# Two-layer diffusion backbone: modulation rows one by one and at 1024 elements, opening and final norm reordered

## The chip, the cores and the metric

The kernel runs on one core of a Trainium2 chip. The metric is the device time of one launch in microseconds (us); lower is better. Each kernel was run three times, and the median is what is compared. Times inside the kernel come from one execution that was recorded by the hardware profiler.

## The reference

Two layers work on 640 tokens of width 1024: 128 context tokens and 512 latents. The even layer mixes tokens with a pooling and a gated convolution, the odd one with grouped-query attention; each is followed by a SwiGLU FFN of inner width 2816. Before each of the four sub-layers stands a norm with a modulation, and its output is gated:

```python
def ada_params(cvec, w_ada, b_ada):
    m = jax.nn.silu(cvec) @ w_ada + b_ada
    return jnp.split(m[:, None, :], 6, axis=-1)
def modulate(x, g, shift, scale):
    return rms_norm(x, g) * (1 + scale) + shift
def swiglu(h, w_in, w_out):
    a, b = jnp.split(h @ w_in, 2, axis=-1)
    return (jax.nn.silu(a) * b) @ w_out
...
    for l in range(DEPTH):
        sh1, sc1, g1, sh2, sc2, g2 = ada_params(c, w_ada[l], b_ada[l])
        h = modulate(x, norm_g[l, 0], sh1, sc1)
        ...
        x = x + g1 * y
        h = modulate(x, norm_g[l, 1], sh2, sc2)
        x = x + g2 * swiglu(h, w_ffn_in[l], w_ffn_out[l])
    y_sample = rms_norm(x, final_g)
```

In the left-out line `y` is the mixer's or the attention's output. Context tokens take their modulation from `c_ctx`, latents from `c`, so each of the 2 x 6 modulation vectors is needed for two conditions. All is float32.

## The kernel before

**Layout.** `x` stays on the core, transposed: 128 partitions, 8 blocks of 128 features, 640 tokens (`T`) in two halves of 320 (`HT`). Each weight block is loaded raw by the one DMA queue that SP issues, in program order, and split in a high and a low part: ScalarE (ACT) makes the high one (L144), VectorE (DVE) the low one (L145). A product of two split operands is three matmuls on TensorE (PE): high-high, high-low, low-high (`THREE`).

**FFN.** The 22 blocks of inner features run in three groups of 8, 8 and 6 (`GROUPS`). A group has an input part (`fi0_0` is layer 0's first) and an output part (`fo0_0`), whose eight steps end with a residual on VectorE (L506). In group 0 four blocks are multiplied plainly (eight steps, L289), the other four, and all of groups 1 and 2, by a scheme with seven products per unit of one block (`fast_blocks`, L630); the last operation of a unit on VectorE before its result is split is L652. A call `each(i)` stands behind step i, `fast_each(gi, n, p)` behind product p of unit n in group gi.

**Modulation rows.** Of the 96 block rows of modulation (2 layers x 6 vectors x 8 blocks) twelve are made on PE, in chunks of four: chunks 2 and 3 (the first sub-layer's scale) and 0 (half of its shift), by `ada_pe` (L306, with the condition as the small operand), `ada_row` (L324, a copy by ACT) and `ada_turn` (L330, tiny matmuls that turn the row into a column, tile `adat`). The other 84 rows are made on VectorE: a row is 128 partitions x 1024 weights (512 KB, tile `rawa`), multiplied with silu of each of the two conditions (`silb`) and summed along the way, in pieces of 512 elements (L371, tile `junk` takes the products): four pieces a row. Rows are jobs of four or eight; behind a job's last row the two halves are added (L385) and a bias is added (L392). `ada` holds 76 rows, `gates` the last 8 (layer 1's FFN gate). `ada.run(n)` puts n rows at that place of the program; the load of a later row follows each row. `EARLY` is the number of rows made before the first FFN; six row buffers there, two later.

**Order.** The opening is written out by hand and emitted in that order on every engine (`manual_schedule`); elsewhere a scheduler places the instructions of each engine by the program's order and its own readiness, but rows are held in program order among the rest (`keep_in_program_order`). On the chip each engine takes its instructions in order.

**Opening.** `prep(k)` makes block k of the first operand, x times scale, in both parts (ACT L483, VectorE L485); blocks 0 to 3 need chunk 2 (`sc`), blocks 4 to 7 chunk 3. `first_mm(m, ks)` multiplies blocks `ks` into output block m of the first projection (`pi`). `nrm.add` squares and sums x for the norm, with `pool_only` both on POOL. L474 is the first VectorE step of that norm behind its row pieces; the norm is applied by the `ev` multiply behind each projection step (L521; L526 copies its last columns on ACT). The pooling mixer follows (L904 and around).

**Tail.** Behind the last projection the final norm is made in two spans of 384 and 256 tokens, then `out` multiplies x with it block by block (L1446), and stores two blocks at a time.

Of the kernel before, what the change touches and what calls it, by code (L numbers as in the profile page):

```python
# [15 lines left out]
P = 128  # L16
D = 1024
# [19 lines left out]
EARLY = 30  # L37
# [23 lines left out]
def hybrid_step(  # L61
# [277 lines left out]
    class AdaDve:  # L339
# [17 lines left out]
        def run(self, rows, hold=True):  # L357
            for _ in range(rows):
# [7 lines left out]
                if b == 0:  # L366
                    self.got = self.rest.tile([P, 8, 2, 2], F32, tag="got", bufs=2, name=f"got_{l}_{b0}")
                for c in range(2):
                    for q in range(2):
                        cols = slice(512 * q, 512 * q + 512)  # L370
# [12 lines left out]
                if b == n - 1:  # L383
                    two = self.got[:, 0:n]
                    V.tensor_tensor(out=two[:, :, :, 0], in0=two[:, :, :, 0], in1=two[:, :, :, 1], op=ALU.add)  # L385
                    ada_done(l, b0, two[:, :, :, 0])
# [114 lines left out]
    def update(m, l, gate0, parts):  # L501

        assert (l, gate0 // 8, 8) in known
# [169 lines left out]
    def ffn(l, xin, hid, each=None, last=None, spare=None, fast_each=None):  # L673
# [37 lines left out]
        for gi, (f0, f1) in enumerate(GROUPS):  # L711
# [21 lines left out]
            if plain:  # L733
                project(f"fi{l}_{gi}", xin, KB, 2 * plain, in_done, ext=True, each=each and (lambda i: each(i, True)))
# [4 lines left out]
            if gi < len(GROUPS) - 1:  # L739
                project(f"fo{l}_{gi}", hid, f1 - f0, KB, lambda k, ps: residual(ps, k, l, 40), each=each)  # L740
# [5 lines left out]
    with tc.tile_pool(name="pool1", bufs=1) as p1:  # L746
# [3 lines left out]
        junk = p0.tile([P, 512], F32, tag="junk", name="junk")  # L750
        ada_raw = []

        def ada_load(ch):
# [8 lines left out]
            [(0, 4, 4)] + [(0, 8 * p, 8) for p in (2, 4, 3, 5)] + [(1, 8 * p, 8) for p in (1, 0, 2, 4, 3)]  # L762
# [5 lines left out]
        nc.sync.dma_start(x[:, 0:4, :], xT[:, 0:4, :])  # L768
        ada_load(3)
        ws.load(1, cut=True)  # L770
# [26 lines left out]

        acc = {ch: ada_acc(ch) for ch in (2, 3)}
        ada_pe(2, acc[2], range(4))
        row = ada_row(2, acc[2])  # L800
        ada_pe(3, acc[3], range(1))
        ada_turn(2, row)
        ada_pe(3, acc[3], range(1, 4))
        for k in range(4):
            nrm.add(k, pool_only=True)
        prep(0, bufA, 0, 0)
        prep(1, bufA, 0, 0)
        prep(2, bufA, 0, 0)
        ws.split(0, ahead=False)
        row = ada_row(3, acc[3])  # L810
        prep(3, bufA, 0, 0)
        ws.split(1, ahead=False)
        first_mm(0, range(0, 2))
        ada_turn(3, row)
        first_mm(0, range(2, 4))
        first_mm(1, range(4))
# [3 lines left out]
        for k in range(4, 8):  # L820
            nrm.add(k)
        first_mm(0, range(4, 8))
        first_mm(1, range(4, 8))
        ada.run(2, hold=False)
# [189 lines left out]
        for m in range(3):  # L1014
# [9 lines left out]
            each=lambda i: ada.run(1 + (i < 7) - (i >= 11)),  # L1024
# [19 lines left out]
        with tc.tile_pool(name="pool4", bufs=1) as p4:  # L1044
# [9 lines left out]
                each=lambda i, plain=False: ada.run(int(i >= 5) if plain else 1 + i % 2),  # L1054
# [550 lines left out]
```

## Time and profile before

| | before |
|---|---|
| runs, us | 1377.27, 1378.74, 1377.84 |
| median, us | 1377.84 |
| profiled execution, us | 1376.99 |
| its span, us | 1375.2 |
| mean granted PE clock | 0.986 |
| busy: PE / PEld / DVE / ACT / POOL | 97% / 94% / 79% / 46% / 5% |
| largest PE groups (share of the ending chain) | fi L630 24%, fo L289 21%, fi L289 7% |
| row pieces L371 | 336 pieces, 237.0 us of VectorE |

PE does matmuls, PEld the loads of their stationary operand. All times below are us from the start of the span, in the form: start, length, engine, line, operation, output <- inputs, shape, count, and in brackets how long the engine was idle before and what ended that.

### The profile page before, as it was taken

The numbers are of one execution on the slowest core, as the hardware profiler recorded it, in microseconds if no ns is written. First come the engines' busy times: TensorE is split into PE (matmuls) and PEld (weight loads), VectorE is DVE, ScalarE is ACT, GpSimd is POOL, SyncE is SP. The second block draws the span as 40 slices with busy tenths as digits, with TensorE's granted clock in tenths as the row PEclk, the third lists the DMA queues.
The fourth block names the chain that finished last, engine by engine and source line by source line (L and its number), as shares of the span: only waits on it lengthen the run. The fifth ranks groups of instructions, "written<-read, shape, count | busy, mean of one in ns | idle before, by whom it ended". The sixth has DMA issues, their size and how long they took to land.

```text
span 1375.2 us, 22538 instructions
## 1 busy us (share of the span) xinstructions
PE 1327.7 (97%) x8929; PEld 1294.1 (94%) x8929; DVE 1081.2 (79%) x2182; ACT 636.3 (46%) x1155; POOL 70.3 (5%) x73
## 2 busy tenths in 40 slices
PE   6989999989999999999999999999999999999995
PEld 3889999989999999999998899999999999999995
DVE  4899988999988898789976777689993577446745
ACT  3532335744135531454565675477551255314543
POOL 3200000000000000000013121000000000000013
PEclk7999999999999999999999999999999999999998
DMA  9635523134533254324531110031242122311212
GB/s 363 250 117 176 195 93 123 64 106 169 172 123 114 95 187 154 108 92 140 188 95 55 43 49 34 32 134 53 106 154 77 62 76 78 123 62 62 77 47 77
DMA packets 36872, 155.54 MB, mean 113 GB/s; under 512 B 4000, under 2 KB 11168, under 8 KB 26016
## 3 DMA queue, kind: packets, MB, share of 16 engines
q1 hardware_dynamic: 36768, 154.12, 32.2%
q8 instruction: 70, 1.15, 0.3%
q14 instruction: 34, 0.28, 0.1%
HBM read 148.60 MB, written 2.88 MB: 110 GB/s over the span
## 4 chain that ended last, share of the span: by engine, by line
PE 77%; DVE 16%; ACT 3%; issue 2%; DMA 1%; SPq 0%; POOL 0%; DVEq 0%; ACTq 0%; POOLq 0%
PE fi L630 24%; PE fo L289 21%; PE fi L289 7%; PE pq L289 5%; PE pi L289 5%; DVE junk L371 5%; PE po L289 4%; DVE wl_fi_p L145 3%; PE wb L289 2%; PE wa L289 2%; PE o L1326 2%; PE s L1276 1%; PE t L1309 1%; ACT wh_fi_p L144 1%; DMA raw_ada<-wada 1%
## 5 line engine op out<-in xcount | busy, mean ns | idle before, releaser
L144 ACT ACTIVATE wh_fi_p<-raw_fi 128x512 fp32r<-128x512 f32 x252 | 153.9, 626 | 219.5 <-PE fi L630 108.6
L371 DVE CUSTOM_DVE_ANT_0 junk<-rawa,silb 128x512 f32<-128x512 f32 x336 | 237.0, 705 | 6.5 <-DMA rawa<-wada 2.2
L145 DVE TENSOR_TENSOR wl_fi_p<-raw_fi,wh_fi_p 128x512 fp32r<-128x512 f32 x252 | 170.1, 686 | 64.1 <-ACT wh_fi_p L144 63.9
L506 DVE SCALAR_TENSOR_TENSOR x<-fo,mod,x 128x128 f32<-128x128 f32 (+1 forms) x144 | 55.5, 433 | 94.1 <-PE fo L289 90.8
L144 ACT ACTIVATE wh_fo<-raw_fo 128x1024 fp32r<-128x1024 f32 (+1 forms) x48 | 47.5, 990 | 145.4 <-PE fo L289 121.2
L630 PE MATMUL fi<-bh,wh_fi_p 128*128 128x320 f32 x288 | 89.0, 309 | 0.7 <-DVE x L506 0.5
L630 PE MATMUL fi<-bh,wl_fi_p 128*128 128x320 f32 x288 | 88.9, 309 | 0.6 <-DVE wl_fi_p L145 0.6
L630 PE MATMUL fi<-ah,wl_fi_p 128*128 128x320 f32 x288 | 88.8, 308 | 0.0
L630 PE MATMUL fi<-al,wh_fi_p 128*128 128x320 f32 x288 | 88.7, 308 | 0.0
L630 PE MATMUL fi<-ah,wh_fi_p 128*128 128x320 f32 x288 | 88.4, 307 | 0.0
L630 PE MATMUL fi<-bl,wh_fi_p 128*128 128x320 f32 x288 | 88.4, 307 | 0.0
L289 PE MATMUL fo<-al,wh_fo 128*128 128x320 f32 x352 | 80.8, 310 | 0.0
L289 PE MATMUL fo<-ah,wh_fo 128*128 128x320 f32 x352 | 80.6, 310 | 0.1
L289 PE MATMUL fo<-ah,wl_fo 128*128 128x320 f32 x352 | 80.4, 309 | 0.0
L289 PE MATMUL fo<-bh,wh_fo 128*128 128x320 f32 x328 | 75.2, 310 | 0.0
L289 PE MATMUL fo<-bh,wl_fo 128*128 128x320 f32 x328 | 75.0, 310 | 0.0
L289 PE MATMUL fo<-bl,wh_fo 128*128 128x320 f32 x328 | 74.9, 310 | 0.0
L630 PE MATMUL fi<-x0h,wh_fi_p 128*128 128x320 f32 x216 | 69.0, 323 | 5.0 <-DVE uv L652 3.6
L630 PE MATMUL fi<-xh,wh_fi_p 128*128 128x320 f32 x216 | 68.0, 320 | 2.6 <-DVE uv L652 2.1
L630 PE MATMUL fi<-x0l,wh_fi_p 128*128 128x320 f32 x216 | 66.9, 311 | 0.0
L630 PE MATMUL fi<-x0h,wl_fi_p 128*128 128x320 f32 x216 | 66.9, 311 | 0.0
L289 PE MATMUL pi<-ah,wh_in 128*128 128x320 f32 (+1 forms) x256 | 62.3, 326 | 4.7 <-ACT ev L526 3.8
(375 smaller groups left out, 3808.7 us busy)
## 6 DMA issues: line engine op xcount, KB each, us to landing
raw_fi<-wfi SPq DMA_DIRECT2D x44, 1024.0 KB, 4.8
rawa<-wada SPq DMA_DIRECT2D x84, 512.0 KB, 3.4
raw_fo<-wfo SPq DMA_DIRECT2D x16, 1024.0 KB, 4.9
raw_ada<-wada SPq DMA_DIRECT2D x12, 512.0 KB, 9.9
raw_in<-win SPq DMA_DIRECT2D x6, 1024.0 KB, 6.4
raw_fo<-wfo SPq DMA_DIRECT2D x8, 768.0 KB, 4.2
raw_qkv<-wqkv SPq DMA_DIRECT2D x6, 1024.0 KB, 5.0
raw_out<-wout SPq DMA_DIRECT2D x4, 1024.0 KB, 4.8
```

The costliest lines, as they stand in the source:

```text
L144: S.activation(h, src, AF.Copy)
L145: eng.tensor_tensor(out=l, in0=src, in1=h.bitcast(F32), op=ALU.subtract)
L289: PE.matmul(ps[:, h, 0 : hi - lo], w[a][:, k, cols], rhs[b][:, k0 + k, lo:hi], start=k == 0 and a == b, stop=k == kn - 1 and a == 1,)
L371: op = V.tensor_tensor_reduce(out=self.junk, in0=raw[:, cols], in1=self.silb[:, c, cols], scale=1.0, scalar=0.0, op0=ALU.mult, op1=ALU.add ...
L506: V.scalar_tensor_tensor(out=xs, in0=got[:, 0 : b - a], scalar=mod[l][:, gate0 + m, c : c + 1], in1=xs, op0=ALU.mult, op1=ALU.add,)
L630: PE.matmul(out, w[a][:, k, :], ops.get(OPERAND[p], b)[:, k, :], start=fresh and k == 0 and a == b, stop=k == ops.kn - 1 and a == 1, skip_ ...
L1276: PE.matmul(self.ps[:, hf, 0:HT], bufB[a][:, self.h, q0 : q0 + P], kt[b][:, self.kv, hf * HT : hf * HT + HT], start=n == 0, stop=n == 2,)
L1309: PE.transpose(flat(pt)[:, s * P : s * P + P], self.pe[:, s * P : s * P + P], ident)
L1326: PE.matmul(po[:, 0 : 2 * P], vt[a][:, self.kv, s * P : s * P + P], got[b][:, s, :], start=s == 0 and n == 0, stop=s == 4 and n == 2,)
```

## The change

- A row is split by the width of the tile that takes the products. The early one is now 1024 wide, so the 28 rows ahead of the first FFN (`EARLY`, 30 before) are two pieces each instead of four and need no addition of halves; later rows keep pieces of 512.
- The rows of the two FFN gate vectors (part 5 of each layer) are jobs of one row: addition and bias follow each row, and a residual asks only for its own block's row.
- Opening: the first projection's weights are loaded ahead of chunk 3's rows; dummy matmuls of zeros (128x512, into a bank that is free then) are put on PE in three places (6, 3 and 14); `ada_turn` of chunk 2 no longer stands behind chunk 3's first matmul; all four first `prep`s come ahead of chunk 3; the squares go from POOL to ACT and their sums from POOL to VectorE.
- FFN of layer 0: no rows in group 0's input part (seven before); fewer and more in the output parts (group 0 as before, `1 + i % 2`; group 1 two a step from the third step on); one in each unit of groups 1 and 2 (in every second before).
- Layer 1: the eight rows of `gates` move from the fast units of group 0 to the steps of `fo1_0`, one each, the first two loads ahead of the FFN.
- Tail: `out` multiplies four blocks in one operation on VectorE (it was one block at a time, a third on POOL) and stores them at once: two stores per span instead of four. The first half of the first span is put ahead of the second span's work. `nrm.finish` there is at raised priority.

```diff
@@ -34,7 +34,7 @@
 PLAIN = 4
 RAW = 3
 
-EARLY = 30
+EARLY = 28
 WINDOWS = (2, 4, 8, 16)
 PAD = 8
 UL = PAD + CTX + PAD + LAT + PAD
@@ -365,9 +365,10 @@
                 self.at += 1
                 if b == 0:
                     self.got = self.rest.tile([P, 8, 2, 2], F32, tag="got", bufs=2, name=f"got_{l}_{b0}")
+                n_part = D // self.junk.shape[-1]
                 for c in range(2):
-                    for q in range(2):
-                        cols = slice(512 * q, 512 * q + 512)
+                    for q in range(n_part):
+                        cols = slice(D // n_part * q, D // n_part * (q + 1))
                         op = V.tensor_tensor_reduce(
...
@@ -382,7 +383,8 @@
                             tc.keep_in_program_order(op)
                 if b == n - 1:
                     two = self.got[:, 0:n]
-                    V.tensor_tensor(out=two[:, :, :, 0], in0=two[:, :, :, 0], in1=two[:, :, :, 1], op=ALU.add)
+                    if n_part == 2:
+                        V.tensor_tensor(out=two[:, :, :, 0], in0=two[:, :, :, 0], in1=two[:, :, :, 1], op=ALU.add)
                     ada_done(l, b0, two[:, :, :, 0])
                 self.load()
 
@@ -500,7 +502,7 @@
...
-        assert (l, gate0 // 8, 8) in known
+        assert any((l, gate0 // 8, n) in known for n in range(m + 1, 9))
...
@@ -731,13 +733,20 @@
                     keep(j, held.pop(j))
 
             if plain:
-                project(f"fi{l}_{gi}", xin, KB, 2 * plain, in_done, ext=True, each=each and (lambda i: each(i, True)))
+                project(f"fi{l}_{gi}", xin, KB, 2 * plain, in_done, ext=True, each=each and (lambda i: each(i, gi, True)))
             if l in FAST:
                 fast_blocks(
                     f"fi{l}_{gi}", list(range(f0 + plain, f1)), ops, plain_keep, lambda j, t: keep(j - f0, t)
                 )
             if gi < len(GROUPS) - 1:
-                project(f"fo{l}_{gi}", hid, f1 - f0, KB, lambda k, ps: residual(ps, k, l, 40), each=each)
+                project(
+                    f"fo{l}_{gi}",
+                    hid,
+                    f1 - f0,
+                    KB,
+                    lambda k, ps: residual(ps, k, l, 40),
+                    each=each and (lambda i: each(i, gi)),
+                )
             else:
                 last(f1 - f0)
 
@@ -747,7 +756,7 @@
-        junk = p0.tile([P, 512], F32, tag="junk", name="junk")
+        junk = p0.tile([P, D], F32, tag="junk", name="junk")
@@ -759,15 +768,18 @@
         ada = AdaDve(
-            [(0, 4, 4)] + [(0, 8 * p, 8) for p in (2, 4, 3, 5)] + [(1, 8 * p, 8) for p in (1, 0, 2, 4, 3)]
+            [(0, 4, 4)]
+            + [(0, 8 * p, 8) for p in (2, 4, 3)]
+            + [(0, 40 + b, 1) for b in range(8)]
+            + [(1, 8 * p, 8) for p in (1, 0, 2, 4, 3)]
         )
         ada.home(p0, p1, 6, junk, silb)
         ada.limit = EARLY
         ada_load(2)
         nc.sync.dma_start(kc, konst)
         nc.sync.dma_start(x[:, 0:4, :], xT[:, 0:4, :])
+        ws.load(1, cut=True)
         ada_load(3)
-        ws.load(1, cut=True)
         nc.sync.dma_start(x[:, 4:8, :], xT[:, 4:8, :])
 
         nc.sync.dma_start(silb, crows[None].broadcast_to((P, 2, D)))
@@ -795,33 +807,50 @@
         def first_mm(m, ks):
             block_mm(first[m], ws.parts[m], bufA, KB, ks=ks)
 
+        idle = first[2][:, 0, :]
+
+        def turn_over(n):
+
+            for _ in range(n):
+                PE.matmul(idle, zeror, zeror2, start=True, stop=True)
+
+        turn_over(6)
         acc = {ch: ada_acc(ch) for ch in (2, 3)}
         ada_pe(2, acc[2], range(4))
         row = ada_row(2, acc[2])
-        ada_pe(3, acc[3], range(1))
+        turn_over(3)
         ada_turn(2, row)
-        ada_pe(3, acc[3], range(1, 4))
+        turn_over(14)
         for k in range(4):
-            nrm.add(k, pool_only=True)
-        prep(0, bufA, 0, 0)
-        prep(1, bufA, 0, 0)
-        prep(2, bufA, 0, 0)
-        ws.split(0, ahead=False)
+            prep(k, bufA, 0, 0)
+            if k == 1:
+                ws.split(0, ahead=False)
+        ws.split(1, ahead=False)
+        for k in range(4):
+            nrm.square(k)
+        first_mm(0, range(4))
+        ada_pe(3, acc[3], range(4))
         row = ada_row(3, acc[3])
-        prep(3, bufA, 0, 0)
-        ws.split(1, ahead=False)
-        first_mm(0, range(0, 2))
+        nrm.add_square(V)
+        nrm.add_square(V)
+        nrm.add_square(V)
+        nrm.add_square(V)
+        first_mm(1, range(2))
         ada_turn(3, row)
-        first_mm(0, range(2, 4))
-        first_mm(1, range(4))
+        first_mm(1, range(2, 4))
         for k in range(4, 8):
             prep(k, bufA, 0, 0)
         S.activation(silb, silb, AF.Silu)
         for k in range(4, 8):
-            nrm.add(k)
+            nrm.square(k)
         first_mm(0, range(4, 8))
         first_mm(1, range(4, 8))
-        ada.run(2, hold=False)
+        ada.run(1, hold=False)
+        nrm.add_square(V)
+        nrm.add_square(V)
+        nrm.add_square(V)
+        nrm.add_square(V)
+        ada.run(1, hold=False)
         ws.split(2, ahead=False)
         ada.run(2, hold=False)
         S.preload_act_table_set("natural_log_exp_and_others")
@@ -1021,7 +1050,7 @@
             13,
             lambda i, ps: mixer_in(i + 3, scaled(ps, f"ev_{i + 3}")),
             ext=True,
-            each=lambda i: ada.run(1 + (i < 7) - (i >= 11)),
+            each=lambda i: ada.run(1 + (5 <= i < 8)),
         )
 
         out_done = updater(0, 16, Norm("a1"), (bufA, 0, 1))
@@ -1051,8 +1080,8 @@
                 0,
                 bufA,
                 bufA,
-                each=lambda i, plain=False: ada.run(int(i >= 5) if plain else 1 + i % 2),
-                fast_each=lambda gi, n, p: ada.run(int(p == 6 and (gi == 0 or n % 2))),
+                each=lambda i, gi, plain=False: ada.run(0 if plain else 1 + (i % 2 if gi == 0 else int(i > 1))),
+                fast_each=lambda gi, n, p: ada.run(int(p == 6 and gi > 0)),
                 last=last0,
                 spare=(tuple(t.rearrange("p a b -> p (a b)") for t in bufB), more),
             )
@@ -1440,13 +1469,13 @@
             nrm.add(k)
             gain(k)
 
-        def out(cols, step):
-            for k in range(KB):
-                xs = x[:, k, cols]
-                (G if k % 3 == 1 else V).tensor_tensor(out=xs, in0=xs, in1=rstd[:, cols], op=ALU.mult)
-                if k % step == step - 1:
-                    ks = slice(k + 1 - step, k + 1)
-                    nc.sync.dma_start(yT[:, ks, cols], x[:, ks, cols])
+        def out(ks, cols):
+            n = cols.stop - cols.start
+            xs = x[:, ks, cols]
+            V.tensor_tensor(
+                out=xs, in0=xs, in1=rstd[:, None, cols].broadcast_to((P, ks.stop - ks.start, n)), op=ALU.mult
+            )
+            nc.sync.dma_start(yT[:, ks, cols], xs)
 
         project("fo1_2", bufA, kn, KB - 2, whole)
         log_exp_tables()
@@ -1468,26 +1497,31 @@
                 parts = [(c, max(a, lo), min(b, hi)) for c, a, b in SEG if a < hi and b > lo]
                 update(KB - 2 + m, 1, 40, [(c, a, b, ps[m][:, h, a - lo :]) for c, a, b in parts])
                 nrm.add(KB - 2 + m, V, cols)
-            nrm.finish((lo, hi), None)
+            with tc.high_priority():
+                nrm.finish((lo, hi), None)
             for m in range(2):
                 gain(KB - 2 + m, cols)
-        for h, (lo, hi) in enumerate(spans):
-            out(slice(lo, hi), 2)
+            if not h:
+                out(slice(0, 4), cols)
+        for h, ks in ((0, slice(4, 8)), (1, slice(0, 4)), (1, slice(4, 8))):
+            out(ks, slice(*spans[h]))
 
     whole_b = tuple(t.rearrange("p a b -> p (a b)") for t in bufB)
     more = tuple(p3.tile([P, 3 * 4 * HT], F32R, tag=t, name=t) for t in ("xh", "xl"))
     silb = p3.tile([P, 2, D], F32, tag="silb", name="silb1")
     nc.sync.dma_start(silb, crows[None].broadcast_to((P, 2, D)))
     S.activation(silb, silb, AF.Silu)
-    gates = AdaDve([(1, 40, 8)], 76)
+    gates = AdaDve([(1, 40 + b, 1) for b in range(8)], 76)
     gates.home(p3, p3, 2, ps_small("junk1"), silb)
+    gates.load()
+    gates.load()
     ffn(
         1,
         bufA,
         bufA,
         last=last1,
         spare=(whole_b, more),
-        fast_each=lambda gi, n, p: gates.run(int(gi == 0 and p in (1, 6))),
+        each=lambda i, gi, plain=False: gates.run(0 if plain or gi else 1),
     )
     assert gates.at == 8
```

The order of PE in the opening, before; `adap_155` and `adap_157` are chunks 2 and 3 in the making, `adat_171` is chunk 2's turn into columns, `pi_152` the first output block of the first projection, and x2 counts adjacent instructions of one form:

```order
6 L306 MATMUL adap_155<-raw_ada_3_103,silc 2x512 x2
7 L306 MATMUL adap_157<-raw_ada_0_107,silc 2x512 x2
8 L330 MATMUL adat_171<-kc,row_167 128x2 x4
9 L306 MATMUL adap_157<-raw_ada_1_109,silc 2x512 x2
10 L306 MATMUL adap_157<-raw_ada_2_111,silc 2x512 x2
11 L306 MATMUL adap_157<-raw_ada_3_113,silc 2x512 x2
12 L289 MATMUL pi_152<-ah,wh_in_0_204 128x320 x2
```

Now, with chunk 2 as `adap_161`, its turn as `adat_178`, chunk 3 as `adap_163`:

```order
7 L306 MATMUL adap_161<-raw_ada_3_103,silc 2x512 x2
8 L815 MATMUL pi_154<-zeror 128x512 x3
9 L330 MATMUL adat_178<-kc,row_173 128x2 x4
10 L815 MATMUL pi_154<-zeror 128x512 x14
11 L289 MATMUL pi_152<-ah,wh_in_0_207 128x320 x2
```

Chunk 3's eight matmuls moved behind the first matmuls of the projection (rows 23 to 26 now, its turn row 33); dummies stand on both sides of chunk 2's turn.

The order of VectorE in the opening between the last `prep` (L485, L487 now) and the norm, before, where a row piece is two rows of the list (the sum and its read-out):

```order
22 L485 SCALAR_TENSOR_TENSOR al<-x,sc_79,ah 128x128
23 L485 SCALAR_TENSOR_TENSOR al<-x,sc_79,ah 128x512
24 L371 ISA junk,got_4_350<-rawa_120,silb 128x512
25 L371 ISA got_4_350 128x1
26 L371 ISA junk,got_4_350<-rawa_120,silb 128x512
27 L371 ISA got_4_350 128x1
28 L371 ISA junk,got_4_350<-rawa_120,silb 128x512
```

And now:

```order
26 L487 SCALAR_TENSOR_TENSOR al<-x,sc_79,ah 128x512
27 L372 ISA junk,got_4_371<-rawa_120,silb 128x1024
28 L372 ISA got_4_371 128x1
29 L372 ISA junk,got_4_371<-rawa_120,silb 128x1024
30 L372 ISA got_4_371 128x1
31 L430 TENSOR_TENSOR ssq_a_151<-ssq_a_151,sq_a_4_315 128x640
32 L430 TENSOR_TENSOR ssq_a_151<-ssq_a_151,sq_a_5_317 128x640
33 L430 TENSOR_TENSOR ssq_a_151<-ssq_a_151,sq_a_6_319 128x640
34 L430 TENSOR_TENSOR ssq_a_151<-ssq_a_151,sq_a_7_321 128x640
35 L372 ISA junk,got_4_371<-rawa_122,silb 128x1024
```

Before, sixteen pieces (rows 24 to 56, one weight split among them) stood there; now eight of twice the width, and four of the sums that POOL made.

The order of VectorE in layer 0's `fi0_0`, ahead of the first unit's L652 (L654 now), before; `got_40` is layer 0's gate, `wl_fi_5_p` a weight's low part, `raw_fi` its loads combined in place:

```order
541 L371 ISA junk,got_40_2004<-rawa_2632,silb 128x512
542 L371 ISA got_40_2004 128x1
543 L145 TENSOR_TENSOR al<-ea_3_2682,ah 128x640
544 L371 ISA junk,got_40_2004<-rawa_2632,silb 128x512
545 L371 ISA got_40_2004 128x1
546 L145 TENSOR_TENSOR wl_fi_5_p_2834<-raw_fi_5_2477,wh_fi_5_p_2833 128x512
547 L242 TENSOR_TENSOR raw_fi_4_2317<-raw_fi_4_2317 128x4x128
548 L652 TENSOR_TENSOR uv<-fi_0_2_2757,uv 128x320
```

And now:

```order
389 L145 TENSOR_TENSOR al<-ea_3_2622,ah 128x640
390 L145 TENSOR_TENSOR wl_fi_5_p_2762<-raw_fi_5_2429,wh_fi_5_p_2761 128x512
391 L145 TENSOR_TENSOR wl_fi_5_p_2762<-raw_fi_4_2269,wh_fi_5_p_2761 128x512
392 L238 TENSOR_TENSOR raw_fi_5_2429<-raw_fi_5_2429 128x4x128
393 L240 TENSOR_TENSOR raw_fi_5_2429<-raw_fi_5_2429 128x4x128
394 L145 TENSOR_TENSOR wl_fi_5_p_2800<-raw_fi_4_2269,wh_fi_5_p_2799 128x512
395 L145 TENSOR_TENSOR wl_fi_5_p_2800<-raw_fi_5_2429,wh_fi_5_p_2799 128x512
396 L654 TENSOR_TENSOR uv<-fi_0_2_2691,uv 128x320
```

The rows are gone from this part, and weight splits for coming products have moved up ahead of that step.

## The prediction

> **What bounds the kernel now.** I read the page first, then the windows of 25 us, PE's waits, the order of time at the places where PE loses time, and the chain for where each stage begins and ends.
>
> ```profile
> span 1375.2 us, 22538 instructions
> PE 1327.7 (97%) x8929; PEld 1294.1 (94%) x8929; DVE 1081.2 (79%) x2182; ACT 636.3 (46%) x1155; POOL 70.3 (5%) x73
> 0.00:25.00 25.00, 13.63 (x46) 3.75 (x46) 8.05 (x10) 8.30 (x14) 11.22 (x15) 0.82 0.95 349
> 75.00:100.00 25.00, 21.24 (x125) 20.79 (x123) 25.00 (x65) 9.00 (x15) 0.33 (x6) 0.86 0.31 106
> 275.00:300.00 25.00, 20.59 (x128) 19.82 (x127) 24.72 (x54) 11.07 (x24) 0.00 (x0) 0.93 0.28 89
> 350.00:375.00 25.00, 25.00 (x172) 25.00 (x171) 24.02 (x64) 4.24 (x4) 0.00 (x0) 1.00 0.57 202
> 1050.00:1075.00 25.00, 25.00 (x172) 25.00 (x171) 9.82 (x17) 3.39 (x4) 0.00 (x0) 1.00 0.23 85
> 1100.00:1125.00 25.00, 24.97 (x169) 24.25 (x168) 18.90 (x31) 13.32 (x26) 0.00 (x0) 1.00 0.24 86
> PE fi L630 <- DVE x L506: 0.5, 1, 0.5
> L371 DVE CUSTOM_DVE_ANT_0 junk<-rawa,silb 128x512 f32<-128x512 f32 x336 | 237.0, 705 | 6.5 <-DMA rawa<-wada 2.2 <-ACT silb L819 1.0
> ```
>
> Columns of a window: PE, PEld, DVE, ACT, POOL busy (instructions), granted clock, DMA share, GB/s. TensorE is the bound, at 97%. It loses time in the opening, where it also runs below full clock (0.82), at 75 to 100 and at 275 to 300, where the clock falls too; in those two VectorE is full (25.00 and 24.72 of 25). In steady stretches PE is full whatever VectorE does. So work taken off VectorE is worth something only where PE waits for it. The rows of L371 are its largest movable part: 336 pieces for 84 rows, four to a row.
>
> **The opening (A).**
>
> ```profile
> 10.68 0.60 ACT L324 ACTIVATE row<-adap 98x512 f32<-98x512 f32 x1 [7.79 <-PE adap L306]
> 13.16 1.25 POOL L436 TENSOR_TENSOR ssq_a<-x 128x640 f32<-128x640 f32 x1 [11.27 <-DMA x<-xT]
> 14.43 1.03 PE L306 MATMUL adap<-raw_ada,silc 128*2 128x512 f32 x4 [3.80 <-DMA raw_ada<-wada]
> 15.38 1.45 PE L330 MATMUL adat<-kc,row 98*128 98x2 f32 x8
> 16.76 3.58 PE L306 MATMUL adap<-raw_ada,silc 128*2 128x512 f32 x12
> 17.30 2.82 ACT L483 ACTIVATE ah<-x,sc 128x128 fp32r<-128x128 f32 x6 [6.03 <-DVE sc L401]
> 26.13 0.90 PE L289 MATMUL pi<-ah,wl_in 128*128 128x320 f32 x2 [3.42 <-DVE wl_in L145]
> 30.57 3.73 ACT L483 ACTIVATE ah<-x,sc 128x128 fp32r<-128x128 f32 x8 [7.02 <-DVE sc L401]
> 36.89 8.03 POOL L440 TENSOR_TENSOR ssq_a<-ssq_a,sq_a 128x640 f32<-128x640 f32 x4 [13.42 <-ACT sq_a L438]
> 43.54 1.92 DVE L371 CUSTOM_DVE_ANT_0 junk<-rawa,silb 128x512 f32<-128x512 f32 x1
> 46.86 1.22 DVE L145 TENSOR_TENSOR wl_in<-raw_in,wh_in 128x1024 fp32r<-128x1024 f32 x1
> 48.72 0.69 DVE L371 CUSTOM_DVE_ANT_0 junk<-rawa,silb 128x512 f32<-128x512 f32 x1
> 49.46 0.69 DVE L371 CUSTOM_DVE_ANT_0 junk<-rawa,silb 128x512 f32<-128x512 f32 x1
> 54.14 0.48 DVE L474 SCALAR_TENSOR_TENSOR ssq_a<-ms_a,ssq_a 128x320 f32<-128x320 f32 x1
> ```
>
> The scale turns (adat, 15.38) stand on PE behind a chunk-3 matmul that waited 3.80 us for its DMA, though their row was ready at 11.28. Now only three dummy matmuls stand there. So the turns, 1.45 long, end near 13.0; scale and shift follow 0.47 later (16.83 to 17.30 before), x has landed at 13.16, and the first prep starts near 13.5 instead of 17.30. Chunk 3 pays: its loads are queued on SP behind 1 MB of win, 3.0 us at 349 GB/s, so its matmuls end at 20.34 + 3.0 = 23.3. The row (0.6), twelve small matmuls (1.8 at 0.147 each, which is 56.54 / 384 from a row below) and turns with scale and shift (about 0.9 more) bring the second prep to about 26.6 instead of 30.57: 4.0 us earlier.
>
> From that prep to L474 VectorE takes 54.14 - 30.57 = 23.6 us. Four row pieces beside POOL's adds (36.89 to 44.92) took about 1.92, as that at 43.54, where 0.69 is normal: 4 x 1.23 = 4.9 go with POOL's work. A piece of 1024 elements isn't in the trace; its nearest row is the 1024 subtraction (1.22). Consecutive pieces start 0.74 apart, so four rows go from 16 x 0.74 = 11.8 to 8 x 1.27 = 10.2, a gain of 1.6 (bounds: 0 if twice 0.69 is the price, 3 if nothing but elements counted). Added: the ssq adds, three of them beside idle time, four here at about 0.74, 3.0. Net 3.5. L474 moves by 4.0 + 3.5 = 7.5 us, to 46.6, and with it the norm, the first ev and the pooling chain. Ends: 4, if the loads of the third and fourth row (asked for only when the first and second are summed) set the pace, 10 if they and chunk 3 land early. I take 7.5, the sum by rows. The squares moved to ACT lie in its 7.02 us wait; the 23 dummies (0.24 each at full clock, 0.47 at half, scaled by columns from 0.147 for 320) lie in PE's 3.80 and 3.42 us waits, and cost what they outlast them.
>
> **The stall at 85 (B).**
>
> ```profile
> 78.66 0.68 DVE L371 CUSTOM_DVE_ANT_0 junk<-rawa,silb 128x512 f32<-128x512 f32 x1
> 79.27 0.84 DVE L904 TENSOR_TENSOR s<-up 128x663 f32<-128x663 f32 x1
> 88.69 0.90 PE L289 MATMUL pi<-ah,wh_in 128*128 128x320 f32 x2 [3.76 <-ACT ev L526]
> 93.13 0.74 PE L289 MATMUL pi<-ah,wl_in 128*128 128x320 f32 x2
> 94.89 0.46 PE L289 MATMUL pi<-ah,wh_in 128*128 128x320 f32 x2
> ```
>
> PE waits 3.76 us for a PSUM tile whose reader, the ev multiply, stands behind row pieces. Then the clock is at half until about 94.2: two matmuls are busy 0.90 to 0.74 us, then 0.46, so 5.5 us hold 5.5 x (1 - 0.46 / 0.82) = 2.4 us of loss. The whole place costs 6.2. Ahead of that ev, since the first window of the pooling, stood twelve pieces, 0.61 each among other work (78.66 to 79.27) and 0.74 in pairs: about 8.0 us. Now five of 1.14: 5.7. The wait falls by 2.3, to 1.5. A wait of 3.76 cost the clock, 0.5 (L506) did not; the remainder is nearer the second, so the 2.4 goes too: 4.7. Ends: 2.3 and 6.2. The Trainium skill (TensorE: Matmul & The Clock Gate, "Part 1: The HAM clock gate") puts the border at one idle window of about 3.4 us, which no wait of this trace tests from below; by it 1.5 us keeps the clock and the term stays 4.7; were the border below 1.5, it would be 2.3.
>
> **The FFN groups without rows (C, D).**
>
> ```profile
> 280.87 1.77 PE fi L630 x12
> 337.54 56.54 PE fo L289 x384
> 1241.21 1.46 PE fi L630 x10
> 1316.75 31.92 PE fo L289 x216
> L624 PE MATMUL fi<-ah,onesr x6: 304/310/388, 973.9 to 1242.8; 128*128 128x320 f32 x6
> 1027.27 56.64 PE fo L289 x384
> 296.35 0.61 PE L630 MATMUL fi<-x0h,wh_fi_p 128*128 128x320 f32 x1 [3.64 <-DVE uv L652]
> ```
>
> Six clean units of seven products last 1316.75 - 1241.21 = 75.5, 12.6 each. Layer 0's first four last 337.54 - 280.87 = 56.7 against 50.4: 6.3 lost, 3.64 of it one wait on L652, which stands on VectorE behind row pieces (the order shows two rows of the same buffer just ahead of it). All rows leave this group, more than the wait, so I take 6.0 back (ends 4 and 6.3; ACT's copies stay). Layer 1's four, from the bias product at 973.9, 0.3 long, to 1027.27, last 53.1: 2.7 lost; its eight rows go to fo1_0, where VectorE is busy 9.82 of 25. Eight rows of about 3 plus two small ops each fit there beside PE. I take 2.3 (1 to 2.7).
>
> **Where the rows go (E).** fo0_0 with 1.5 rows per step of 7.07 us held 24.02 busy, fo1_0 without rows 9.82: (24.02 - 9.82) / 5.3 rows = 2.7 us a row. In fo0_1 the last six steps now hold two: 2.8 + 5.4 = 8.2 in 7.07, so VectorE comes up to 6.7 us late into group 2. Three PSUM tiles and splits made ahead cover most of it; before, the same edge cost 0.5 on L506. In the units VectorE needs 18.90 per 25, 9.5 per unit; one row in each makes 12.2 of 12.6. I take 0.5 lost (ends: 0.5 gained, 6 lost). The added adds and biases of single gate rows, about 0.3 a row, are in it. Each row's load moves with it on SP; the order has one between consecutive raw_fi loads, two buffers ahead.
>
> **The tail (F).**
>
> ```profile
> 1362.17 4.83 DVE L1446 TENSOR_TENSOR x<-x,rstd 128x384 f32<-128x384 f32 x5
> 1368.15 3.35 DVE L1446 TENSOR_TENSOR x<-x,rstd 128x256 f32<-128x256 f32 x5
> rawa<-wada SPq DMA_DIRECT2D x84, 512.0 KB, 3.4
> yT<-x SPq DMA_DIRECT2D x4, 256.0 KB, 2.3
> ```
>
> DVE and POOL share sixteen multiplies; DVE alone now does four. By the 1024 row, 1536 elements are about 1.75, so 3.4 instead of 4.83 and, for 1024, 2.4 instead of 3.35: 2.3 gained. The last store is 512 KB instead of 256: 3.4 against 2.3, 1.1 back. I take 1.0 (-0.5 to 2.3). The raised priority of the norm leaves the order there as it was: nothing.
>
> **Sum.** 7.5 + 4.7 + 6.0 + 2.3 - 0.5 + 1.0 = 21.0. The profiled execution took 1376.99; minus 21.0 is 1356.0. The median of the runs, 1377.84, is 0.85 above it, so 1356.8.
>
> **Rivals.**
> R1: PE opens cold all the same. At half clock the fourteen dummies are 6.6 us instead of 3.3; chunk 3 and the turns, in order behind them, come about 3 us later, and if the stall at 85 also stays over its border, 2.4 more: 1362.2. For it: 0.82 in the first window, and a matmul pair of 0.90 at 26.13; against: PE has no long wait left there. By the Trainium skill (same page and section) about 3.4 us of sustained work opens the clock; the dummies would then do.
> R2: VectorE's lateness at the edge of group 2 isn't covered; it costs 6 instead of 0.5: 1362.3. For it: 8.2 in 7.07. Against: the three tiles, and only 0.5 lost there before.
> R3, slower: each moved row waits for its load, which stands on SP behind a raw_fi load that waits for its own buffer, and VectorE, in order, waits with it. L371 waited 2.2 us for DMA in all before. To undo 21.0 over the fourteen units of groups 1 and 2 it takes 1.5 us a unit beyond the slack; with waits of 2.2 in each and 0.4 slack, 25 us are lost: 1382.
> R4: the opening is set by transfers, not order: A is 1 and B 2.3: 1365.7. For it: DMA share 0.95. Against: the bytes ahead of x's second half are the same.
>
> **How the numbers follow.** Forecast 0.57, R1 0.17, R2 0.10, R4 0.10, R3 0.06. The range 1349 to 1366 leaves out R3; below it ends where all upper ends together (28.0) would, 1349.8; it takes in R1, R2 and R4. A change under 0.2% (2.8 us) couldn't be told from none; a partial R3 may end there. Faster 0.92, same 0.03, slower 0.05.
>
> **What would show it.** L474 near 46.6 and prep at 13.5 and 26.6; row pieces of 1024 near 1.22; no half clock near 90; group 0 of layer 0 in 50 to 51 us, layer 1's the same; groups 1 and 2 within 1 us of before; stores two by two, with DVE's multiplies at 1.75 and 1.22. I'm wrong if groups 1 or 2 show waits on L652 or rawa in every unit, or if the opening stays at half clock past 30.

## The result, and the profile after

The changed kernel took 1358.45 us (median of four runs, 1353.84 to 1359.17) against 1377.55 before (four runs as well): a ratio of 0.9853, with an interval of 0.983 to 0.9875. That is 19.1 us less; 21.0 had been forecast (1356.8, range 1349 to 1366). The profiled execution took 1359.17 us.

The head of the page after, and four windows of 25 us (columns as in the windows of before):

```profile
span 1357.0 us, 22469 instructions
PE 1327.6 (98%) x8952; PEld 1295.8 (95%) x8952; DVE 1076.8 (79%) x2095; ACT 638.5 (47%) x1159; POOL 46.3 (3%) x56
0.00:25.00 25.00, 21.86 (x108) 13.29 (x109) 9.39 (x16) 10.85 (x18) 1.31 (x8) 1.00 0.96 353
25.00:50.00 25.00, 22.77 (x127) 19.31 (x127) 20.36 (x40) 12.80 (x20) 0.00 (x0) 0.86 1.04 391
75.00:100.00 25.00, 22.86 (x144) 22.59 (x143) 23.02 (x41) 9.79 (x15) 0.33 (x6) 0.93 0.32 108
275.00:300.00 25.00, 24.98 (x169) 24.31 (x168) 19.12 (x30) 12.79 (x25) 0.00 (x0) 1.00 0.24 85
```

VectorE's and TensorE's busy times are nearly what they were. The stretch at 275 is full now. The opening starts at full clock, but 25 to 50 and 75 to 100 still lose some of it (0.86 and 0.93). The first of these dips is new: from 37.5 to 50 the clock was full before. Before, then after:

```profile
37.50:50.00 12.50, 11.70 (x81) 9.48 (x80) 12.23 (x20) 5.42 (x8) 7.17 (x4) 1.00 0.30 97
37.50:50.00 12.50, 10.67 (x47) 9.74 (x48) 10.27 (x22) 4.75 (x7) 0.00 (x0) 0.73 1.03 408
```

The chain gives the starts of the stages after; where layer 1's fast units begin is read from the order of time (the fourth row):

```profile
271.38 22.92 PE fi L632 x156
321.40 56.54 PE fo L289 x384
615.44 42.50 PE fo L289 x288
959.90 0.45 PE L626 MATMUL fi<-ah,onesr 128*128 128x320 f32 x2
1010.54 56.64 PE fo L289 x384
1300.05 31.91 PE fo L289 x216
```

The two starts of before that weren't shown:

```profile
630.17 42.50 PE fo L289 x288
973.95 0.45 PE L624 MATMUL fi<-ah,onesr 128*128 128x320 f32 x2
```

Each stage is the difference of two neighbouring starts; the other starts of before stand in the prediction:

| stage | before | after | difference | forecast |
|---|---|---|---|---|
| start to layer 0's fast units (A, B) | 280.87 | 271.38 | -9.49 | -12.2 |
| `fi0_0`'s fast units (C) | 56.67 | 50.02 | -6.65 | -6.0 |
| `fo0_0` to `fi0_2` (E) | 292.63 | 294.04 | +1.41 | +0.5 |
| `fo0_2` to the end of `fi1_0`'s plain steps | 343.78 | 344.46 | +0.68 | 0 |
| `fi1_0`'s fast units (D) | 53.32 | 50.64 | -2.68 | -2.3 |
| `fo1_0` to `fi1_2` | 289.48 | 289.51 | +0.03 | 0 |
| `fo1_2` to the end (F) | 58.45 | 56.95 | -1.50 | -1.0 |

The sum is -18.20, the difference of the two profiled spans. The order of time after shows the steps of the opening:

```profile
12.84 1.93 ACT L485 ACTIVATE ah<-x,sc 128x128 fp32r<-128x128 f32 x4 [1.93 <-DMA x<-xT]
25.70 3.74 ACT L485 ACTIVATE ah<-x,sc 128x128 fp32r<-128x128 f32 x8 [2.54 <-DVE sc L403]
32.54 1.22 DVE L372 CUSTOM_DVE_ANT_0 junk<-rawa,silb 128x1024 f32<-128x1024 f32 x1
33.69 3.61 DVE L430 TENSOR_TENSOR ssq_a<-ssq_a,sq_a 128x640 f32<-128x640 f32 x4
46.05 0.48 DVE L476 SCALAR_TENSOR_TENSOR ssq_a<-ms_a,ssq_a 128x320 f32<-128x320 f32 x1
40.90 0.90 PE L289 MATMUL pi<-ah,wl_in 128*128 128x320 f32 x2 [1.09 <-DVE wl_in L145]
41.60 1.70 PE L330 MATMUL adat<-kc,row 98*128 98x2 f32 x8
43.16 0.88 PE L289 MATMUL pi<-ah,wh_in 128*128 128x320 f32 x2
47.04 0.73 PE L289 MATMUL pi<-al,wh_in 128*128 128x320 f32 x2
47.93 0.46 PE L289 MATMUL pi<-ah,wh_in 128*128 128x320 f32 x2
57.80 0.71 ACT L926 ACTIVATE up<-ev 128x512 f32<-128x512 f32 x1
80.93 0.56 PE L289 MATMUL pi<-ah,wh_in 128*128 128x320 f32 x2 [2.14 <-ACT ev L528]
82.00 0.74 PE L289 MATMUL pi<-ah,wh_in 128*128 128x320 f32 x2
85.53 0.46 PE L289 MATMUL pi<-al,wh_in 128*128 128x320 f32 x2
```

The preps came at 12.84 and 25.70, a wide piece takes 1.22, and L476 (L474 before) came at 46.05: 8.1 us earlier. But `up`, the first step of the pooling, stands at 57.80; before it stood here:

```profile
63.94 0.72 ACT L897 ACTIVATE up<-ev 128x512 f32<-128x512 f32 x1
```

So only 6.1 of the 8.1 us reached the pooling. What is late in between is TensorE: from 40.90 to 47.9 its pairs of matmuls take 0.73 to 0.90 us instead of 0.46, and the product for the norm's second half stands behind them. The wait ahead of the fourth projection step fell from 3.76 to 2.14, and half clock follows it, from 82.00 to 85.2.

### The profile page after: what moved, and what is told of

It is laid out like the page before. It is cut to its first block, busy times and chain, and to the rows that moved or that the text cites. A ratio compares the mean times of both kernels' runs of the same rounds, so it can differ in the third digit from the quotient of the medians.

```text
span 1357.0 us, 22469 instructions
## 1 busy us (share of the span) xinstructions
PE 1327.6 (98%) x8952; PEld 1295.8 (95%) x8952; DVE 1076.8 (79%) x2095; ACT 638.5 (47%) x1159; POOL 46.3 (3%) x56
## 3 DMA queue, kind: packets, MB, share of 16 engines
q8 instruction: 70, 1.15, 0.3%
## 4 chain that ended last, share of the span: by engine, by line
PE 82%; DVE 11%; ACT 3%; issue 2%; DMA 1%; SPq 0%; POOL 0%; DVEq 0%; ACTq 0%; POOLq 0%
PE fi L632 28%; PE fo L289 19%; PE fi L289 8%; PE pi L289 7%; PE pq L289 5%; PE po L289 4%; DVE junk L372 3%; PE wb L289 2%; PE wa L289 2%; PE o L1355 2%; PE s L1305 2%; DVE wl_fi_p L145 1%; PE t L1338 1%; ACT wh_fi_p L144 1%; DMA x<-xT 1%
## 5 line engine op out<-in xcount | busy, mean ns | idle before, releaser
L372 DVE CUSTOM_DVE_ANT_0 junk<-rawa,silb 128x512 f32<-128x512 f32 (+1 forms) x280 | 224.1, 800 | 5.9 <-DMA rawa<-wada 1.7
L632 PE MATMUL fi<-xh,wl_fi_p 128*128 128x320 f32 x216 | 66.5, 309 | 0.0
L632 PE MATMUL fi<-xl,wh_fi_p 128*128 128x320 f32 x216 | 66.5, 309 | 0.0
```

The source lines that it names most:

```text
L372: op = V.tensor_tensor_reduce(out=self.junk, in0=raw[:, cols], in1=self.silb[:, c, cols], scale=1.0, scalar=0.0, op0=ALU.mult, op1=ALU.add ...
L632: PE.matmul(out, w[a][:, k, :], ops.get(OPERAND[p], b)[:, k, :], start=fresh and k == 0 and a == b, stop=k == ops.kn - 1 and a == 1, skip_ ...
```

## The experiments

Theory: the time came from the places of the table, each edit from its own. What is missing of A and B (2.7 us) went to TensorE's clock, which fell behind waits of 0.3 to 2.1 us. Rivals: VectorE still sets the opening; the dummies or the wide pieces carry it; the clock falls for reasons other than TensorE's empty time.

**The old order of the opening.** The part from the first chunk to the early rows as before, with wide pieces.

```diff
-        ws.load(1, cut=True)
         ada_load(3)
+        ws.load(1, cut=True)
...
-        turn_over(3)
+        ada_pe(3, acc[3], range(1))
         ada_turn(2, row)
...
+            nrm.add(k, pool_only=True)
```

> The changed kernel with the opening in the order of before (chunk 3's loads ahead of the weights, chunk 2's turn behind chunk 3's first matmul, squares and sums on POOL, no dummies); pieces of 1024, 28 early rows and all the rest as changed. Theory: the order carries the opening. In the trace the step from the first norm to the pooling came 6.1 us earlier, of which the wide pieces can be 16 x 0.74 - 8 x 1.24 = 1.9; so this kernel is 4 to 6 us slower than the changed one, and its cold clock and POOL's slowing of row pieces are back. Rival: the wide pieces carry it and the order is hidden; then it is less than 2 us slower.

It took 1361.50 us (1360.40 to 1362.72; ratio to before 0.9879, 0.9866 to 0.9893), 3.05 above the changed kernel, where 4 to 6 was expected. In its order of time:

```profile
62.10 0.72 ACT L909 ACTIVATE up<-ev 128x512 f32<-128x512 f32 x1
39.77 2.47 DVE L372 CUSTOM_DVE_ANT_0 junk<-rawa,silb 128x1024 f32<-128x1024 f32 x1
85.24 0.56 PE L289 MATMUL pi<-ah,wh_in 128*128 128x320 f32 x2 [2.15 <-ACT ev L528]
85.93 0.46 PE L289 MATMUL pi<-ah,wl_in 128*128 128x320 f32 x2
```

The pooling starts at 62.10: the order, with its dummies, carries 4.3 of the 6.1 us. Wide pieces beside POOL's adds take 2.47 instead of 1.22, as the narrow ones took 1.92 instead of 0.69. In the profiled execution the loss shrinks from 4.3 to 2.8 by the start of layer 0's fast units, and the last two rows show where: here the same wait of 2.15 us left the clock up (0.46 behind it), which after 2.14 it did not.

**Narrow pieces in the new opening.**

```diff
-        junk = p0.tile([P, D], F32, tag="junk", name="junk")
+        junk = p0.tile([P, 512], F32, tag="junk", name="junk")
```

> The changed kernel with early row pieces of 512 elements, four to a row. Theory: a wide piece saves only the second start: 1.9 us ahead of the norm (16 x 0.74 against 8 x 1.24) and some 0.7 on the wait at 79 (ten pieces of 0.64 against five of 1.14); 2 to 3 us slower than the changed kernel, more if the longer wait at 79 keeps the clock down longer. Rival: VectorE isn't what sets the opening's end; then no difference (within 0.7).

1358.11 us (1356.82 to 1359.65; 0.9854, 0.9841 to 0.9868): no difference from the changed kernel. The theory missed. In its order of time:

```profile
47.39 0.48 DVE L476 SCALAR_TENSOR_TENSOR ssq_a<-ms_a,ssq_a 128x320 f32<-128x320 f32 x1
57.19 0.71 ACT L926 ACTIVATE up<-ev 128x512 f32<-128x512 f32 x1
80.09 0.70 PE L289 MATMUL pi<-ah,wh_in 128*128 128x320 f32 x2 [1.92 <-ACT ev L528]
```

VectorE reaches L476 1.3 us later than in the changed kernel, but in this execution TensorE's half clock was shorter (from 42.6 to 46.3), and the pooling starts 0.6 earlier. So the two effects can't be told apart here. The wait ahead of the fourth step isn't longer (1.92 against 2.14): there the pieces stand singly among other work, 0.61 for a narrow one and 1.14 for a wide one, and the width brings next to nothing.

**No dummies.**

```diff
-        turn_over(6)
...
-        turn_over(3)
...
-        turn_over(14)
```

> The changed kernel without the 23 matmuls of zeros in the opening. Theory: they keep TensorE's clock up; without them the first matmuls of the projection (15.77 to 20 now) and chunk 3's run at half clock, chunk 3's turn comes 2 to 3 us later, and the kernel is 1.5 to 3 us slower, with a granted clock below 0.9 in the first 25 us (1.00 now). Rival: chunk 3's loads set the second prep (its matmuls wait for DMA anyway); then the clock falls but the time stays within 0.5 us.

1359.11 us (1356.74 to 1360.16; 0.9859, 0.9846 to 0.9873), 0.7 above the changed kernel, which the runs don't separate; 1.5 to 3 was expected. In the profiled execution the clock is lower where it was expected, and the pooling's `up` came at 59.37, 1.6 later:

```profile
12.50:25.00 12.50, 9.14 (x49) 7.12 (x50) 8.96 (x15) 8.62 (x15) 0.00 (x0) 0.73 1.06 393
```

So the existing dummies hold the clock in the opening, at a worth between nothing and 1.6 us.

**More dummies where TensorE waits.**

```diff
         nrm.finish((0, HT), None)
+        turn_over(9)
         first_mm(2, range(0, 1))
...
+            if g == 0:
+                for _ in range(8):
+                    PE.matmul(warm, zeror, zeror2, start=True, stop=True)
```

> The changed kernel with 9 more matmuls of zeros ahead of the third first_mm (38.2 us) and 8 behind the first pooling product (78.6 us), both in places where TensorE waits. Theory: the two stretches at half clock (40.9 to 47.9 and 82.0 to 85.2) come from TensorE's empty time just before them; filled, they run at full clock: 7.0 x 0.45 + 3.2 x 0.45 = 4.6 us less, if both lie on the path. Rival: the clock is dropped for another reason, or VectorE sets the path at both places; then no gain, or up to 1 us lost by dummies that outlast the wait.

1353.95 us (1353.68 to 1354.79; 0.9825, 0.9812 to 0.9839): 4.5 us less than the changed kernel, where 4.6 was expected, and its runs lie within 1.1 us, the changed kernel's within 5.3. Windows and order of time of this kernel:

```profile
37.50:50.00 12.50, 11.93 (x80) 10.45 (x81) 11.25 (x25) 6.32 (x11) 0.00 (x0) 1.00 1.03 410
75.00:87.50 12.50, 12.19 (x78) 11.52 (x77) 12.50 (x23) 6.14 (x10) 0.33 (x6) 1.00 0.47 158
46.42 0.81 PE L466 MATMUL ms_a<-ssq_a,ones 128*128 128x320 f32 x2 [0.56 <-DVE ssq_a L476]
76.51 1.99 PE L972 MATMUL warm<-zeror 128*128 128x512 f32 x8
78.80 0.55 PE L289 MATMUL pi<-ah,wh_in 128*128 128x320 f32 x2 [0.31 <-ACT ev L528]
```

The clock is at 1.00 in both (0.73 and 0.86 in the changed kernel). Nothing else was changed, so the two dips came from TensorE's empty time. Their price is less sure than the 4.5 suggests: of the 5.0 us between the two profiled executions, 2.1 are there at the pooling's start (55.68 against 57.80) and 3.65 at the start of layer 0's fast units; the rest fell behind it, in stages that the edit doesn't touch. The fastest run of the changed kernel, 1353.84 at a mean clock of 0.996 (0.992 or 0.993 in its other runs), lies where this kernel lies. Now VectorE is awaited at 46.42.

The next five kernels, and the narrow pieces at full clock, stand on this one, since its runs spread less. They ran later; the kernel of before, run beside each group, had medians from 1377.48 to 1378.11, so a difference of less than about 0.6 us says nothing.

**Layer 0's rows back in group 0.** With them the output part of group 1 and the units of groups 1 and 2 get fewer rows again.

```diff
-                each=lambda i, gi, plain=False: ada.run(0 if plain else 1 + (i % 2 if gi == 0 else int(i > 1))),
-                fast_each=lambda gi, n, p: ada.run(int(p == 6 and gi > 0)),
+                each=lambda i, gi, plain=False: ada.run(int(i >= 5) if plain else 1 + i % 2),
+                fast_each=lambda gi, n, p: ada.run(int(p == 6 and (gi == 0 or n % 2 or (gi == 2 and n < 4)))),
```

> The changed kernel with the 17 more zero matmuls of the kernel that came out at 1353.95 us, and layer 0's FFN rows where they were before: three behind the last plain steps and one in each unit of group 0, 1 + i % 2 in the output parts, every second unit of group 1, five of six units of group 2 (the two rows that were early before). Theory: group 0's input part lost its time to VectorE's rows (56.7 us before, 50.0 now) and the wait at group 2's edge grew by 1.3 from the doubled rows ahead of it; so this is 6.6 - 1.3 = 5.3 us slower than 1353.95. Rival: the weight splits of group 0 on ACT set it, and the gain had come from elsewhere; then within 1 us.

1360.55 us (1359.07 to 1361.24; 0.987, 0.9852 to 0.9887): 6.6 slower than 1353.95, where 5.3 was expected. Group 0's fast units take 57.8 us instead of 50.0, and 1.0 comes back between there and `fi0_2`. The wait on the unit's last VectorE step is there again:

```profile
283.44 0.61 PE L632 MATMUL fi<-x0h,wh_fi_p 128*128 128x320 f32 x1 [3.92 <-DVE uv L654]
```

**Layer 1's gates back in group 0.**

```diff
-        each=lambda i, gi, plain=False: gates.run(0 if plain or gi else 1),
+        fast_each=lambda gi, n, p: gates.run(int(gi == 0 and p in (1, 6))),
```

> The same kernel of 1353.95 us with layer 1's eight gate rows in the units of group 0, two each, as before. Theory: 2.9 us slower, all between the start of that group's units and the output part (53.4 us before, 50.5 now). Rival: the schedule around it hides the rows now that they are single jobs; then within 0.7 us.

1357.62 us (1357.25 to 1357.75; 0.9849, 0.9834 to 0.9865): 3.7 slower, where 2.9 was expected; `fi1_0`'s fast units take 54.3 instead of 50.7. TensorE's waits in it have a row that the kernel of 1353.95 has only at 0.2:

```profile
PE fi L632 <- DVE uv L654: 3.0, 3, 1.5
```

**The old tail.**

```diff
...
-            if not h:
-                out(slice(0, 4), cols)
-        for h, ks in ((0, slice(4, 8)), (1, slice(0, 4)), (1, slice(4, 8))):
-            out(ks, slice(*spans[h]))
+        for h, (lo, hi) in enumerate(spans):
+            out(slice(lo, hi), 2)
```

> The same kernel of 1353.95 us with the final multiplies one block at a time on VectorE and POOL, two blocks a store, behind the second span's work, as before. Theory: 1.5 us slower (from the last projection to the end 58.45 before, 56.95 now), since sixteen multiplies beside POOL take 4.8 + 3.4 where four take 3.3 + 2.4, less what the smaller last store gives back. Rival: the last store sets the end; then no slower or faster by up to 1 us.

1356.02 us (1355.39 to 1356.14; 0.9837, 0.9822 to 0.9853): 2.1 slower. From the start of the last projection to the end its trace gives the 1.5 expected (58.45 against 56.96); its opening was 0.6 later in that execution.

**Rows early in `fo0_1`.**

```diff
-                each=lambda i, gi, plain=False: ada.run(0 if plain else 1 + (i % 2 if gi == 0 else int(i > 1))),
+                each=lambda i, gi, plain=False: ada.run(0 if plain else 1 + (i % 2 if gi == 0 else int(i < 6))),
```

> The same kernel of 1353.95 us with the two rows a step of the second output part in its first six steps and one in the last two, instead of one in the first two and two in the last six. Theory: the wait on the last residual at group 2's edge (1.35 us here, 0.48 before the change) is VectorE's lateness; two steps of 5.5 us work in 7.07 let it catch up, so the wait falls to 0.5 or less: 0.9 to 1.4 us faster. Rival: the rows' loads set it (the two buffers are refilled behind weight loads); then VectorE waits for them earlier and nothing is won, or up to 1 us lost.

1354.53 us (1354.23 to 1355.01; 0.9828, 0.9812 to 0.9843): no gain where 0.9 to 1.4 was expected. The wait stayed (1.35 before this edit), and VectorE waited only 0.5 us in all for loads of rows, so the rival doesn't explain it:

```profile
PE fi L632 <- DVE x L508: 1.5, 1, 1.5
```

**No row in the last step of `fo0_1`.**

```diff
-                each=lambda i, gi, plain=False: ada.run(0 if plain else 1 + (i % 2 if gi == 0 else int(i > 1))),
+                each=lambda i, gi, plain=False: ada.run(0 if plain else 1 + (i % 2 if gi == 0 else int(i < 7) - int(i == 7))),
```

> The kernel of 1353.95 us with two rows in each of the first seven steps of the second output part and none in the last. Theory: in the last step row pieces stand between the three parts of the last residual (533.7 to 536.1, of which 1.3 is its own) and TensorE's next product waits for its bank; without them the three end by about 534, the wait of 1.35 us goes, and the kernel is 1.2 us faster. The miss of the front-loaded rows speaks for this: there one row still stood in the last step. Rival: VectorE comes late into the last step in any case (2 x 2.7 + 2.8 in 7.07 us), so the residual starts late by as much; then within 0.4 us.

1352.90 us (1352.39 to 1353.67; 0.9823, 0.981 to 0.9836), 1.05 faster than 1353.95 and the lowest of all; 0.3 of that may be drift, since before was lower by as much in this group. The trace has 0.9 of it in the right place, from `fo0_0` to `fi0_2` (292.8 against 293.6). Its waits of TensorE, with those of the kernel of 1353.95 ahead:

```profile
PE fi L632 <- DVE x L508: 1.4, 1, 1.4
PE fi L632 <- ACT fi L644: 0.9, 1, 0.9
```

```profile
PE fi L632 <- DVE x L508: 1.1, 1, 1.1
PE fi L632 <- ACT fi L644: 0.4, 1, 0.4
```

The wait on the last residual fell by only 0.2 against the 1.35 of the kernel it stands on, the next one by 0.6. So the theory got the gain nearly right but its place only in part: most of the wait on the residual stays, as the rival had it, and what went is mostly the wait behind it. That VectorE comes late into the last step, and that the rows there delayed what follows, fits both rows but wasn't tested further.

**Narrow pieces at full clock.** The `junk` tile of the second experiment, in the kernel of 1353.95.

> The kernel of 1353.95 us with early row pieces of 512. Theory: in the changed kernel the narrow pieces cost nothing because TensorE, at half clock from 40.9 to 47.9, came after VectorE; here TensorE runs at full clock and its second norm product waits 0.56 us for VectorE, so VectorE's extra 1.9 us ahead of the norm, less what slack there is, shows: 1 to 2 us slower. Rival: the pieces have no place on the path even then; within 0.4 us.

1355.52 us (1354.55 to 1355.83; 0.984, 0.9827 to 0.9854): 1.6 slower, the pooling starts 2.0 later (57.72), and the wait that was 0.56 is

```profile
48.47 0.81 PE L466 MATMUL ms_a<-ssq_a,ones 128*128 128x320 f32 x2 [1.55 <-DVE ssq_a L476]
```

The clock is at 1.00 in both kernels, so this is the clean comparison: the wide pieces bring their time where TensorE isn't itself late.

**The first nine dummies alone.** The edit of the fourth experiment without the second place.

> The changed kernel with only the 9 zero matmuls at 38 us. Theory: each stretch at half clock costs its own loss: the first 7.0 x 0.45 = 3.1, the second 3.2 x 0.45 = 1.4. So this kernel gains 3 us on the changed one and stays 1.4 us above 1353.95, in those runs in which the wait at 77 costs the clock; the runs spread more than with both. Rival: only the first stretch lies on the path; then it equals 1353.95 within 0.4 us.

1354.62 us (1353.65 to 1359.48; 0.9842, 0.9827 to 0.9857), 0.7 above 1353.95 and spread over 5.8 us. In the profiled execution the second dip stands (clock 0.86 from 75 to 87.5, behind a wait of 2.13); three of the other runs, with a mean clock of 0.996, seem to have been without it. The run of 1359.48, at a mean clock of 0.992, lost more than the 1.4 that was expected of the second dip; where is open, as it has no profile. In the profiled executions the first place brings 2.5 of the 3.65 us, the second 1.15.

## Why the prediction was right, and where it was off

**The total** is nearer than its terms. By the profiled spans, 18.2 us against 21.0, A, B and E fell short by 3.6 us together, 0.7 was lost in stages without a forecast, and C, D and F gave 1.5 more than forecast. That these 1.5 offset part of the rest is luck.

**A, 7.5 forecast, 6.1 measured.** L474's place (46.6 forecast, 46.05 measured) and the wide piece (1.22) came as worked out; of the 8.1 us the prep gave 4.9 (4.0 forecast) and VectorE's row of work 3.2 (3.5). The step that failed is "and with it the norm, the first ev and the pooling chain": behind the norm's step stood TensorE at half clock, a dip that wasn't there before. With dummies there the pooling started at 55.68, 8.3 us earlier than before. That the wide pieces save 1.6 was right at full clock (1.6 measured); in the changed kernel itself it didn't show in the time.

**B, 4.7 forecast, 3.35 measured** (9.49 less 6.14). The wait fell by 1.6 instead of 2.3. The twelve pieces of before were priced at 8.0, partly as pairs; they all stood singly, at 0.61 each, which is 7.3, and five of 1.14 from that leaves the 1.6:

```profile
77.10 1.22 DVE L372 CUSTOM_DVE_ANT_0 junk<-rawa,silb 128x1024 f32<-128x1024 f32 x1
78.24 0.83 DVE L933 TENSOR_TENSOR s<-s 128x649 f32<-128x649 f32 x1
```

Most of it is that two and a half rows stand there instead of three. The width gives 0.4 of it at most (ten narrow pieces would be 6.1), and with narrow pieces the wait was 1.92. The step that failed is "the remainder is nearer the second, so the 2.4 goes too": 2.14 us of waiting still cost half clock, and 1.4 of the 2.4 stayed (six pairs from 82.00 to 85.21, 0.535 apart instead of 0.295). So its sign "no half clock near 90" didn't hold. The forecast took a border between 0.5 and 3.76 (before also had a wait of 1.54, ahead of the norm's product at 54.68, that left the clock up); a wait of 2.1 is neither safe nor lost, since it cost the clock after and not in the old order. The rule cited in the prediction, from the Trainium skill (TensorE: Matmul & The Clock Gate, "Part 1: The HAM clock gate"), would have kept the clock at 2.14; the measurement decides. The same section also says that the window runs freely and the moment of a change varies with it. The spread from run to run fits that, but no run here shows the window.

**C, 6.0 forecast, 6.65 measured, and D, 2.3 forecast, 2.7 measured.** Both were held below what stood above the clean units; all of it came back (50.0 and 50.6 against 50.4). Putting the rows back cost 7.8 and 3.6 in these units, 6.6 and 3.7 in the whole kernel.

**E, 0.5 forecast, 1.4 measured.** The lateness of VectorE was seen; the step that failed is that the tiles cover all but 0.5 of it. The wait on the last residual grew from 0.48 to 1.81:

```profile
PE fi L632 <- DVE x L508: 1.8, 1, 1.8
```

With the same code there it was 1.35 in the kernel of 1353.95, so part of this is scatter. In the units themselves one row in each cost nothing, and VectorE waited 1.7 us in all for loads of rows (2.2 before): R3, the slower rival, did not come, and R2 came in small.

**F, 1.0 forecast, 1.5 measured.** The multiplies took what was forecast (2.4 us less in all), and the larger store gave back 0.9 of it, not 1.1; the forecast's own 2.3 less 1.1 is 1.2, which it took as 1.0:

```profile
1345.46 3.42 DVE L1475 TENSOR_TENSOR x<-x,rstd 128x1536 f32<-128x1536 f32 x2
1350.04 2.36 DVE L1475 TENSOR_TENSOR x<-x,rstd 128x1024 f32<-128x1024 f32 x2
```

R1 priced a colder opening, and without the dummies it showed (0.73), at 0 to 1.6 us instead of 3; of its second part, the 2.4 behind the stall, 1.4 came. R4 did not come. The 0.68 us from `fo0_2` through `fi1_0`'s plain steps, where no edit lies, stay open: the part up to the first plain step took 286.4 before, 287.1 after and 286.05 to 287.0 in the first four experiments, all with the same code there, so most of it looks like scatter of that stage.

## What to carry to other kernels

Work taken off an engine is worth what the next late engine leaves of it: follow each gain to the next wait, and ask whether TensorE runs at full clock when it gets there. Where TensorE waited 1 to 2 us ahead of a large product, a few matmuls of zeros in the wait kept the clock here; seventeen of them took 4.5 us off the median, where the whole change brought 19.1. Work that isn't urgent should stand where VectorE has slack, and not in the last step ahead of an edge at which TensorE needs VectorE's result.

## What was not expected of the hardware

- Ahead of the fourth projection step, waits of TensorE of 1.92 to 2.15 us were followed by half clock for 3 to 4 us in four profiled executions, and by none in a fifth (2.15 us). Earlier in the changed kernel, three shorter ones in a row (0.28, 0.74, 1.09 us, with matmuls of two columns around them) were followed by 7 us of it.
- A row piece beside POOL's additions takes about 1.2 us longer, whatever its width: 2.47 us instead of 1.22 for 1024 elements, 1.92 instead of 0.69 for 512.
- A row piece of 1024 elements replaces two of 512. Back to back it saves 0.2 us (starts 1.27 apart against twice 0.74); singly among other work, where the next instruction starts 1.14 us behind a wide piece and 0.61 behind a narrow one, it saves less than 0.1.
